# Delta rule: a 16-bit first correction of the triangular inverse, and decay columns as the bias of the exponential

## The chip, the cores and the metric

The kernel runs on one core of one Trainium2 chip. The metric is the device time of one execution in microseconds, as a median of several runs. Five engines work side by side: TensorE (PE in the profile, with its weight loads as PEld), VectorE (DVE), ScalarE (ACT), GpSimd (POOL), and SyncE (SP), which issues the DMA transfers.

## What is computed

One layer of an encoder trunk handles 2048 frames of a new stream ("prompt") and 64 frames of a running one ("sample"), 1024 channels wide. After a norm comes one input projection. One part of its columns feeds a gated delta rule with 4 heads of 128 channels, another a pooling group. Then come an output projection with a residual, a second norm, a SwiGLU feed-forward block and a last norm. The change is inside the delta rule, of which the reference says:

```
G = jnp.cumsum(g, axis=-1)
gamma = jnp.exp(jnp.where(lower_incl, G[..., :, None] - G[..., None, :], -jnp.inf))
kb = k * beta[..., None]
Lm = jnp.where(lower_strict, jnp.einsum('bhncd,bhnsd->bhncs', kb, k) * gamma, 0.0)
T = lax.linalg.triangular_solve(eye + Lm, eye, left_side=True, lower=True)
u = jnp.einsum('bhncs,bhnsv->bhncv', T, v * beta[..., None])
w = jnp.einsum('bhncs,bhnsk->bhnck', T, kb * jnp.exp(G)[..., None])
qk = jnp.einsum('bhncd,bhnsd->bhncs', q, k) * gamma
```

For each chunk of frames it needs the matrix gamma of decay factors, whose exponent is a difference of a row value and a column value of the running sum G, and the inverse T of a triangular matrix. The state is then carried from chunk to chunk.

## The kernel before, in words

**Two phases.** Phase 1 runs from the start to about 1000 us: input projection, delta rule, pooling and output projection, over four blocks of 512 prompt frames (block 0 also takes the 64 sample frames). Phase 2 is the feed-forward block, and nothing in it is touched.

**The large matrix products.** In phase 1, `project` (line 787) and `out_proj` (line 1289) multiply with three products for each pair of tiles, since weights and activations are split into a high and a low part (`wsplit`, line 529; type F32R). Their results lie in the PSUM tiles pp and pz, which rotate over PSM = 3 banks. VectorE (in block 0) or ScalarE (in the other blocks) brings the projection's results out of PSUM in `evict` (line 779).

**Fronts.** Each head of each block has two `Front` objects (line 868) of two 128-frame chunks each: 4 blocks x 4 heads x 2 = 32, and one more for the four sample heads together (`h is None`). A front prepares everything that doesn't depend on the running state, in `all` (line 921):

- keys are transposed and normed (tiles ptk, ktl, kn)
- `rowmm` (line 897) writes the row values of G into a PSUM bank, tile gb; ScalarE takes the exponential EG of it (line 948)
- onto the same bank go a mask by a bf16 matmul with idbf (line 955) and, by `negmm` (line 908), the negative column values: two F32R matmuls, for each chunk one, with seln as the moving operand. ScalarE's exponential of that, two chunks in one instruction, is Gam (line 961)
- GpSimd takes the identity off (Gst), and the products of keys and queries in bank gr are multiplied in (lines 965 to 972)
- the inverse is built up over seven levels in 16-bit arithmetic (tiles Um, py, Yt, pt, TV; lines 979 to 1001). Levels 0, 2 and 4 write a tile with the tag TV0, levels 1, 3 and 5 one with the tag TV1, and the last writes TV32 in 32 bits, with T and V as its halves
- two corrections follow. The residual F (tile pf and line 1008) is multiplied with V into bank px0, and T = V + that (lines 1010 to 1013); then F is multiplied with the new T into px1, and X = V + that (lines 1016 to 1020). These four matmul calls for each front have 32-bit operands. px0 and px1 are both shown as px_p (px_s for the sample front) in the profile.

**Heads.** `Head` (line 1032) then carries the state through the chunks (tiles pk, rhs, vn, po) and norms the result (osq, os). At most NLEV = 3 fronts have a set of level tiles and a bank at the same time.

**What sets the order.** Every instruction is first noted by `Machine` (line 59) with an estimated duration and then put in order by a greedy list scheduler, `issue` (line 183), for all engines at once. Fronts and heads are "hot" and go ahead of projection work. On TensorE, `pick` (line 281) takes 16-bit and plain 32-bit matmuls ahead of F32R ones, and holds them back for a moment while F32R work is at hand. Since it ranks by estimates, any change of the instructions can shift the order elsewhere too. All instructions of the program are issued from line 278, so the profile's groups are told apart by their tiles.

**Rows.** `rows` (line 1137) computes G and its exponentials for each block. A matmul with sel12 puts the running sums, frames on partitions, into the PSUM tile pc, and one exponential (line 1174) makes the tile EC from it.

The names with __ and a number in the profile are the same tiles, numbered.

## Time and profile before

| what | us |
|---|---|
| median of 3 runs | 2386.49 (2385.48 to 2387.06) |
| profiled execution | 2391.23 |
| its span, from first to last instruction | 2389.5 |
| TensorE busy | 2347.9 |
| VectorE busy | 1681.2 |
| ScalarE busy | 1217.8 |
| GpSimd busy | 971.1 |

The busy time of TensorE counts overlapped, modelled ends of matmuls, so it says where TensorE had something in hand, not that it ran at its peak. What one group of matmuls really takes is seen from the start of the group to the start of the next.

### The profile page before, as it was taken

The numbers are of one execution on the slowest core, as the hardware profiler recorded it, in microseconds if no ns is written. First come the engines' busy times: TensorE is split into PE (matmuls) and PEld (weight loads), VectorE is DVE, ScalarE is ACT, GpSimd is POOL, SyncE is SP. The second block draws the span as 40 slices with busy tenths as digits, with TensorE's granted clock in tenths as the row PEclk, the third lists the DMA queues.
The fourth block names the chain that finished last, engine by engine and source line by source line (L and its number), as shares of the span: only waits on it lengthen the run. The fifth ranks groups of instructions, "written<-read, shape, count | busy, mean of one in ns | idle before, by whom it ended". The sixth has DMA issues, their size and how long they took to land.

```text
span 2389.5 us, 41681 instructions
## 1 busy us (share of the span) xinstructions
PE 2347.9 (98%) x14803; PEld 2183.0 (91%) x14803; DVE 1681.2 (70%) x2963; ACT 1217.8 (51%) x2746; POOL 971.1 (41%) x1146
## 2 busy tenths in 40 slices
PE   9999999999999999999999999999999999999998
PEld 8999798778887878899999999999899999999998
DVE  7999875785577786787776763767566657666466
ACT  6666654564456464574454554553333554434334
POOL 1656442554356652264332226454233464222111
PEclk9999999999999999999999999999999999999999
DMA  7644566455555575999876778976755697566763
GB/s 267 224 166 137 184 224 220 143 168 189 177 184 177 165 192 171 320 370 338 294 284 225 280 264 260 309 260 238 278 192 178 199 350 247 174 211 210 260 207 115
DMA packets 228448, 540.57 MB, mean 226 GB/s; under 512 B 28304, under 2 KB 86672, under 8 KB 228240
## 3 DMA queue, kind: packets, MB, share of 16 engines
q1 hardware_dynamic: 228240, 537.92, 66.8%
q8 instruction: 116, 1.90, 0.3%
q14 instruction: 92, 0.75, 0.1%
HBM read 389.41 MB, written 148.41 MB: 225 GB/s over the span
## 4 chain that ended last, share of the span: by engine, by line
PE 83%; DVE 8%; ACT 3%; DMA 2%; issue 2%; POOL 1%; SPq 0%; DVEq 0%; POOLq 0%; ACTq 0%
PE px L278 19%; PE pp L278 14%; PE pz L278 12%; PE py L278 10%; PE d L278 8%; PE dx L278 6%; PE dy L278 3%; PE pk_p L278 2%; PE pt_p L278 1%; PE dz L278 1%; PE gr_p L278 1%; DVE y L278 1%; PE px_p L278 1%; DVE Yqk L278 1%; PE py_p L278 1%
## 5 line engine op out<-in xcount | busy, mean ns | idle before, releaser
L278 PE MATMUL pp<-h,wsp 128*128 128x512 f32 (+1 forms) x2480 | 562.1, 366 | 3.9 <-DVE h L278 2.8
L278 PEld LDWEIGHTS pp<-h,wsp 128*128 128x128 f32 x2480 | 402.6, 190 | 52.0 <-DVE h L278 3.9
L278 POOL TENSOR_TENSOR Um_p<-Gst_p,lmask 128x256 f16<-128x256 f32 x224 | 179.0, 813 | 108.1 <-PE py_p L278 79.3
L278 PE MATMUL pz<-op,wsp 128*128 128x512 f32 (+1 forms) x960 | 216.7, 366 | 2.5 <-ACT op L278 2.0
L278 PEld LDWEIGHTS pz<-op,wsp 128*128 128x128 f32 x960 | 155.8, 190 | 22.5 <-ACT op L278 2.5
L278 PE MATMUL d<-h,wsd 128*128 128x352 f32 x1056 | 169.6, 322 | 0.0
L278 PEld LDWEIGHTS d<-h,wsd 128*128 128x128 f32 x1056 | 168.3, 188 | 0.5 <-DVE h L278 0.5
L278 DVE TENSOR_TENSOR TV_p<-TV_p,pt_p 128x512 f16<-128x512 f16 (+1 forms) x192 | 128.5, 681 | 48.4 <-PE pt_p L278 43.1
L278 PE MATMUL px<-hA,ws 128*128 128x352 f32 x792 | 141.9, 324 | 0.3 <-DMA ws<-g 0.3
L278 PE MATMUL pz<-hB,ws 128*128 128x352 f32 x792 | 139.9, 322 | 0.3 <-DMA ws<-g 0.3
L278 PE MATMUL py<-hB,wsS 128*128 128x352 f32 x792 | 139.1, 322 | 0.3 <-ACT u L278 0.3
L278 PE MATMUL px<-hBT,wsS 128*128 128x352 f32 x792 | 137.6, 322 | 1.9 <-ACT g L278 1.9
L278 PE MATMUL px<-hBT,ws 128*128 128x352 f32 x792 | 137.9, 322 | 1.5 <-DVE u L278 1.5
L278 PE MATMUL px<-hA,wsS 128*128 128x352 f32 x792 | 137.4, 322 | 0.9 <-ACT g L278 0.9
L278 POOL TENSOR_TENSOR wrS<-wr,wrS 128x512 f32<-128x512 f32 x44 | 62.9, 1430 | 185.4 <-DMA wrS<-in_wu_dram 61.2
L278 PE MATMUL py<-hA,wsS 128*128 128x352 f32 x792 | 137.4, 322 | 0.0
L278 ACT ACTIVATE hr<-g 128x352 f32<-128x352 f32 x132 | 65.7, 498 | 132.3 <-DVE g L278 131.9
L278 PEld LDWEIGHTS px<-hBT,wsS 128*128 128x128 f32 x792 | 128.2, 188 | 2.5 <-ACT g L278 2.5
L278 PEld LDWEIGHTS px<-hA,ws 128*128 128x128 f32 x792 | 129.8, 189 | 0.7 <-DMA ws<-g 0.6
L278 PEld LDWEIGHTS px<-hBT,ws 128*128 128x128 f32 x792 | 128.0, 188 | 2.3 <-DVE u L278 2.1
L278 PEld LDWEIGHTS px<-hA,wsS 128*128 128x128 f32 x792 | 128.3, 188 | 1.2 <-ACT g L278 1.2
L278 PEld LDWEIGHTS pz<-hB,ws 128*128 128x128 f32 x792 | 128.7, 188 | 0.6 <-issue 0.6
(690 smaller groups left out, 5499.8 us busy)
## 6 DMA issues: line engine op xcount, KB each, us to landing
wsS<-gS SPq DMA_DIRECT2D x176, 512.0 KB, 4.7
ws<-g SPq DMA_DIRECT2D x132, 512.0 KB, 4.7
wsp<-wnd SPq DMA_DIRECT2D x126, 512.0 KB, 3.5
gS<-wsS SPq DMA_DIRECT2D x88, 512.0 KB, 5.3
g<-ws SPq DMA_DIRECT2D x66, 512.0 KB, 5.3
wnd<-wsp SPq DMA_DIRECT2D x42, 512.0 KB, 4.7
xd<-x2d SPq DMA_DIRECT2D x96, 176.0 KB, 4.0
wrd<-in_wd_dram SPq DMA_DIRECT2D x56, 256.0 KB, 4.3
```

The lines of the kernel that those rows point to most:

```text
L278: getattr(getattr(self.nc, op.eng), name)(*args, **kw)
```

## The change

Three things change.

1. In each prompt front the two `negmm` matmuls are dropped. The mask matmul closes the bank. The exponential that makes Gam becomes two ScalarE instructions of one chunk each, which take the negative column values as a bias of one value for each partition.
2. The bias comes from a new tile NG of each block: one more ScalarE instruction in `rows` copies the running sums out of pc with the factor -1. The sample front keeps its `negmm`.
3. In every front, the sample's too, ScalarE makes 16-bit copies of V and F in a tile VF, which has the tag TV0. The first correction (px0) multiplies these copies. The second (px1) still multiplies 32-bit operands.

```
-            else:
-                for c in range(2):
-                    at = self.off + c * C
-                    mm(ps[:, c * C : (c + 1) * C], G[:, at : at + C], seln[:, self.h, :].to_broadcast([P, C]),
-                       start=False, stop=c == 1, skip_group_check=True)
...
-            dd = gb if self.h is not None else self.ps(f"dd_{tag}")
-            mm(dd[:, : 2 * C], idbf, bc(negm2 if self.h is None else negm, 2, C), start=dd is not gb, stop=False,
-               skip_group_check=dd is gb)
-            self.negmm(dd)
-            if dd is not gb:
+            Gam = self.QKG = gt([P, 2, C], F32, "Gam", NOUT)
+            if self.h is None:
+                dd = self.ps(f"dd_{tag}")
+                mm(dd[:, : 2 * C], idbf, bc(negm2, 2, C), start=True, stop=False)
+                self.negmm(dd)
                 self.rowmm(dd, False)
-            Gam = self.QKG = gt([P, 2, C], F32, "Gam", NOUT)
-            act(Gam, two(dd), AF.Exp)
+                act(Gam, two(dd), AF.Exp)
+            else:
+                mm(gb[:, : 2 * C], idbf, bc(negm, 2, C), start=False, stop=True, skip_group_check=True)
+                for c in range(2):
+                    act(Gam[:, c], two(gb)[:, c], AF.Exp, bias=self.B.NG[:, self.c0 + c, self.h : self.h + 1])
...
             tt(F, F, two(pf), ALU.subtract)
+            VF = lev(F16, "TV0", "w", [P, 2, 2, C])
+            nc.scalar.copy(VF[:, 0], V)
+            nc.scalar.copy(VF[:, 1], F)
             yield LAT_F
             px = self.ps(f"px0_{tag}")
             for c in range(2):
-                mm(px[:, c * C : (c + 1) * C], F[:, c], V[:, c], start=True, stop=True)
+                mm(px[:, c * C : (c + 1) * C], VF[:, 1, c], VF[:, 0, c], start=True, stop=True)
...
-        act(EC[:, :nch, :], pc[:, : 12 * nch].rearrange("p (c t) -> p c t", t=12), AF.Exp)
+        pcs = pc[:, : 12 * nch].rearrange("p (c t) -> p c t", t=12)
+        act(EC[:, :nch, :], pcs, AF.Exp)
+        NG = B.NG = gp.tile([P, 4, NH], F32, tag="NG", name=f"NG{j}", bufs=2)
+        act(NG[:, :nch], pcs[:, :, :NH], AF.Copy, scale=-1.0)
```

More of the change, by code (lines that the diff above doesn't have):

```diff
@@ L910, in negmm @@
             G = self.B.Ghl
-            if self.h is None:
-                for h in range(NH):
-                    mm(ps[:, h * DEC : (h + 1) * DEC], G[:, SO : SO + P], seln[:, h, :].to_broadcast([P, DEC]),
-                       start=False, stop=False)
-            else:
-                for c in range(2):
-                    at = self.off + c * C
-                    mm(ps[:, c * C : (c + 1) * C], G[:, at : at + C], seln[:, self.h, :].to_broadcast([P, C]),
-                       start=False, stop=c == 1, skip_group_check=True)
+            for h in range(NH):
+                mm(ps[:, h * DEC : (h + 1) * DEC], G[:, SO : SO + P], seln[:, h, :].to_broadcast([P, DEC]),
+                   start=False, stop=False)
         def all(self):
```

## Prediction

> **What bounds the kernel now.** I read the page first: the share of each engine, the slices, the chain that ended last.

> ```profile
> span 2389.5 us, 41681 instructions
> ...
> PE 2347.9 (98%) x14803; PEld 2183.0 (91%) x14803; DVE 1681.2 (70%) x2963; ACT 1217.8 (51%) x2746; POOL 971.1 (41%) x1146
> ...
> PE 83%; DVE 8%; ACT 3%; DMA 2%; issue 2%; POOL 1%; SPq 0%; DVEq 0%; POOLq 0%; ACTq 0%
> ```

> TensorE has something in hand for 98% of the span and carries 83% of the last chain. An average can hide stages, so next come the stretches of phase 1, where all fronts lie (columns: stretch, its length, busy us of PE, PEld, DVE, ACT, POOL, clock, DMA share, GB/s).

> ```profile
> 50.00:250.00 200.00, 196.54 (x1579) 181.78 (x1578) 187.95 (x377) 128.02 (x335) 117.91 (x169) 1.00 0.55 182
> 250.00:480.00 230.00, 227.75 (x1492) 193.78 (x1491) 159.63 (x292) 127.22 (x312) 97.35 (x136) 1.00 0.59 190
> 480.00:710.00 230.00, 229.52 (x1366) 183.93 (x1365) 153.98 (x272) 117.75 (x297) 102.38 (x141) 1.00 0.54 176
> 710.00:876.00 166.00, 161.54 (x989) 130.26 (x987) 130.60 (x220) 102.74 (x258) 112.22 (x143) 1.00 0.57 179
> 876.00:970.00 94.00, 91.01 (x517) 73.17 (x517) 67.61 (x127) 45.91 (x113) 23.57 (x30) 0.98 0.64 184
> ```

> TensorE is without work for 3.5, 2.3, 0.5, 4.5 and 3.0 us of these, 13.6 us of 920. From 250 on, VectorE has a fifth to a third free, ScalarE 38% and more, and the DMA engines over a third. The first stretch, block 0, is different: VectorE is busy for 187.95 of 200 us there. A TensorE that gets faster soon meets VectorE in that stretch, and nowhere else. Who makes TensorE wait between 250 and 876 is in its waits (us in total, times, longest):

> ```profile
> PE pk_p L278 <- DVE Sp L278: 1.7, 1, 1.7
> PE pt_p L278 <- ACT Yt_p L278: 0.9, 2, 0.5
> PE gb_p L278 <- ACT ktl_p L278: 0.9, 2, 0.5
> ```

> These are the three longest, 3.5 us in 626. While a front waits for its next step, projection matmuls fill TensorE. So the fronts' own latency is covered, and time that is taken off TensorE should come off the span.

> **What the edits take off TensorE.** Durations of matmuls overlap, so I take start to start, from the order of time on TensorE (start, us, group, count):

> ```profile
> 668.41 0.28 PE L278 MATMUL py_p<-TV_p,Um_p 128*128 128x128 f16 x2
> 668.53 0.66 PE L278 MATMUL pf_p<-TV_p,Gst_p 128*128 128x128 f32 x4
> 669.03 0.27 PE L278 MATMUL gb_p<-negm,idbf 128*128 128x256 bf16 x1
> 669.06 0.41 PE L278 MATMUL gb_p<-seln,Ghl 128*128 128x128 f32 x2
> 669.31 1.16 PE L278 MATMUL pp<-h,wsp 128*128 128x512 f32 x4
> 670.30 1.03 PE L278 MATMUL gr_p<-Yqk 128*128 128x256 f32 x4
> 671.17 0.27 PE L278 MATMUL pt_p<-Yt_p,TV_p 128*128 128x128 f16 x2
> 671.28 0.28 PE L278 MATMUL pt_p<-TV_p,Yt_p 128*128 128x128 f16 x2
> 671.39 0.66 PE L278 MATMUL px_p<-TV_p,F_p 128*128 128x128 f32 x4
> 671.81 0.47 PE L278 MATMUL pp<-h,wsp 128*128 128x512 f32 x1
> ...
> 938.98 0.28 PE L278 MATMUL pt_p<-TV_p,Yt_p 128*128 128x128 f16 x2
> 939.07 1.18 PE L278 MATMUL pz<-op,wsp 128*128 128x512 f32 x4
> 940.09 0.38 PE L278 MATMUL pk_p<-Sp,Yqk 128*128 128x128 f32 x2
> ```

> *Column values.* A pair of seln matmuls takes 669.06 to 669.31, 0.25 us. Not all of it goes. Four projection matmuls that follow such a pair take 0.99 us (669.31 to 670.30), four that follow a 16-bit pair 1.02 (939.07 to 940.09): the seln pair already pays 0.03 us of the turn to F32R that the next matmul pays without it. That leaves 0.22 us for a pair; bounds 0.22 and 0.25.

> *First correction.* The pair of 32-bit products runs as four matmuls and takes 671.39 to 671.81, 0.42 us. Pairs of the same size in 16 bits take 0.12 (668.41), 0.11 (671.17) and 0.09 us (938.98). The difference is 0.30 to 0.33; I take 0.31.

> ```profile
> L278 PE MATMUL px_p<-TV_p,F_p 128*128 128x128 f32 x256 | 40.7, 279 | 1.8 <-DVE F_p L278 1.1 <-DVE TV_p L278 0.5
> L278 PE MATMUL gb_p<-seln,Ghl 128*128 128x128 f32 x64 | 14.2, 307 | 0.0
> ```

> 64 seln matmuls are 32 pairs: 32 x 0.22 = 7.0 us (to 8.0). The 256 of px_p are two corrections of 32 fronts at four each; one of the two becomes 16-bit, and the sample front's too: 33 x 0.31 = 10.2 us (9.9 to 10.9). Together 17.2 us (16.9 to 18.9).

> **What they add, and where it lies.** ScalarE gets a second exponential for each prompt front, two casts for each front, and one copy for each block. The nearest rows:

> ```profile
> L278 ACT ACTIVATE Gam_p<-gb_p 128x256 f32<-128x256 f32 x32 | 12.2, 385 | 1.6 <-PE gb_p L278 1.4
> L278 ACT ACTIVATE vn_p<-pk_p,kn_p 128x128 f32<-128x128 f32 x64 | 23.6, 369 | 45.2 <-PE pk_p L278 45.1
> L278 ACT CAST Yt_p<-py_p 128x256 f16<-128x256 f32 x192 | 68.5, 371 | 111.8 <-PE py_p L278 111.1
> L278 ACT CAST wsd<-wrdl 128x256 fp32r<-128x256 f32 x36 | 14.6, 406 | 33.0 <-PE dx L278 25.5 <-PE py L278 7.0
> L278 ACT ACTIVATE EC<-pc x4: 205/211/211, 42.9 to 724.5; 128x48 f32<-128x48 f32 x4
> ```

> Two instructions like vn_p (one value for each partition, 128 wide) less one like Gam: 2 x 369 - 385 = 353 ns, an upper end, since neighbours overlap. Casts are shown with a 16-bit output from PSUM (371) and with an SBUF source (406); the new ones have both traits, so 66 x 0.37 to 0.41. NG is as EC, 4 x 0.21. In all 11.3 + 24.4 to 27.1 + 0.8 = 37 to 39 us. In the five stretches ScalarE was busy for 521.6 of 920 us, 57%; that becomes 61%. I cost it at nothing on the way to the end: what hides it is the projection work that TensorE does meanwhile. VectorE, GpSimd, the DMAs and SP's queue get nothing and are passed by nothing.

> In a front, the cast of F (0.41) stands in the chain, and its product is 0.31 shorter. V's cast can run while pf is made. The second exponential adds at most 0.35 ahead of Gst on GpSimd, and the 0.25 of the seln pair is gone. So a front becomes 0.1 us longer by the first and up to 0.1 by the second. Behind a cast that waits for F on ScalarE's queue stand its other casts, the SiLU exponentials and the evictions that free the three pp banks. F is made by one VectorE instruction:

> ```profile
> L278 DVE TENSOR_TENSOR F_p<-F_p,pf_p 128x256 f32<-128x256 f32 x32 | 13.2, 414 | 3.4 <-PE py_p L278 1.6 <-PE pf_p L278 1.3 <-POOL F_p L278 0.4
> ```

> A wait of about that length, 0.4 us, is short beside a bank, which 24 projection matmuls fill in 24 x 0.25 = 6 us (1.02/4 for one). If the cover were gone, 32 x 0.2 = 6 us would be the price of the longer chain.

> [...]

> **The sum.** Block 0 holds nine fronts, eight and the sample's: 8 x 0.53 + 0.31 = 4.6 us come off TensorE where VectorE is 94% busy. TensorE would need 192 us for this stretch and VectorE 188, with waits for one another in between. I take half as lost, 2.3 us (bounds 0 and 4.6). The schedule is put in order anew, and fronts are a little longer; on 13.6 us of waits I add 1 (bounds -2 and 5). 17.2 - 2.3 - 1 = 13.9 us. The profiled execution took 2391.2 us, 1.7 of it outside the span, and would take 2377.3. It is 4.7 above the median of the three runs, and I take the same 13.9 off the median 2386.5: 2372.6 us. The bounds together give 18.9 + 2 = 20.9 and 16.9 - 4.6 - 5 = 7.3 us, so 2365.6 to 2379.2.

> **The rivals.**

> *Partly eaten.* The greedy order is drawn anew and waits grow by half of the 13.6 us: 17.2 - 4.6 - 6.8 = 5.8 us, 2380.7. For it: durations in the scheduler are estimates, and block 0 is tight. Against it: the waits are few and scattered, no single one recurs.

> *No change.* TensorE isn't really the bound, and the matmuls taken out were covered: 2386.5. [...] Doubled waits (17.2 - 4.6 - 13.6 = -1) would come to the same time.

> *Slower.* ScalarE sets the pace: its queue is in order, and each front's 1.15 us (37 to 39 over 33) delays Yt, the evictions or the silu behind it, so that TensorE runs dry. Wholly uncovered that is 38 - 17.2 = 21 us more, 2407; with three quarters uncovered 28 - 17 = 11, 2398. It turns slower once 17.2/38, 45%, is uncovered. For it: ScalarE is the engine that gets work, and seven levels of each front pass through it by Yt. Against it: ScalarE waited for TensorE and not the other way round (111 us before Yt against 0.9 us of TensorE for Yt between 250 and 876).

> **Chances.** A measurement of this kernel can tell about 0.2%, 4.8 us, from no change: faster is below 2381.7, slower above 2391.3. My forecast, in its bounds, has 0.68; partly eaten 0.15; still more gained than the bounds say 0.03; no change 0.09; slower 0.05. The first three make 0.86 for faster. The range is 2365 to 2382, the forecast's bounds and the partly eaten case.

> **What would show it.** Right: the group gb_p from seln is gone; px_p splits into 128 32-bit and 64 16-bit matmuls, TensorE has 64 + 66 fewer (14803 to 14673), and ScalarE 32 + 66 + 4 more (2746 to 2848); a 16-bit pair of px takes about 0.11 us from start to start; the stretch after block 0, with 24 fronts, shrinks by about 24 x 0.53 = 12.7 us, and block 0 by some 2; phase 2, from the first px<-hA on, is as long as before; TensorE's waits for px_p and Gst stay under a microsecond or two. Wrong: waits of TensorE for Yt, pp banks or px_p that recur front by front; a phase 2 of another length; block 0 as long as before with more waits for VectorE; or new 16-bit groups that take 0.2 us and more.

## The result and the profile after

| | before | after |
|---|---|---|
| median of 12 runs, us | 2387.86 (2385.48 to 2391.02) | 2384.09 (2381.23 to 2388.95) |
| profiled execution, its span, us | 2391.23, 2389.5 | 2387.10, 2385.3 |
| granted clock of the profiled execution | 0.996 | 0.993 |

The ratio is 0.9983, with a 95% interval of 0.9976 to 0.9991: 3.8 us or 0.17% faster, where 13.9 us were forecast. That is just inside what I had called no change, and 2 us above the range.

The page of after, its span and its engines:

```profile
span 2385.3 us, 41505 instructions
...
PE 2339.3 (98%) x14673; PEld 2168.3 (91%) x14673; DVE 1674.2 (70%) x2963; ACT 1246.9 (52%) x2848; POOL 968.7 (41%) x1146
```

The instructions are as forecast: 14673 on TensorE, 2848 on ScalarE, and ScalarE's busy time is up by 29 us, where 37 to 39 were reckoned. The groups (mean ns of one behind the busy us):

```profile
L278 ACT ACTIVATE Gam_p<-gb_p,NG 128x128 f32<-128x128 f32 x64 | 20.1, 374 | 1.8 <-PE gb_p L278 1.7
L278 PE MATMUL px_p<-TV_p,F_p 128*128 128x128 f32 x128 | 20.0, 279 | 0.2 <-DVE TV_p L278 0.2
L278 ACT CAST TV0w_p<-F_p 128x256 f16<-128x256 f32 x32 | 13.1, 410 | 13.9 <-DVE F_p L278 13.7
L278 ACT CAST TV0w_p<-TV_p 128x256 f16<-128x256 f32 x32 | 13.0, 406 | 11.4 <-DVE TV_p L278 11.3
L278 PE MATMUL px_p<-TV0w_p 128*128 128x128 f16 x64 | 9.0, 222 | 0.0
```

The seln group is gone and the first correction is 16-bit. TensorE never waited for it (0.0 us before px_p<-TV0w_p). So the work did leave TensorE. Where the time went is in the same stretches of phase 1 as before (length, busy us of PE, PEld, DVE, ACT, POOL, clock, DMA share, GB/s):

```profile
50.00:250.00 200.00, 193.41 (x1523) 177.22 (x1522) 185.65 (x374) 133.88 (x359) 118.33 (x172) 0.98 0.53 180
250.00:480.00 230.00, 229.60 (x1490) 194.40 (x1489) 160.50 (x302) 136.18 (x341) 94.88 (x136) 1.00 0.57 194
480.00:710.00 230.00, 229.36 (x1369) 183.62 (x1368) 154.91 (x278) 128.89 (x328) 106.89 (x147) 1.00 0.54 178
710.00:876.00 166.00, 161.53 (x940) 127.44 (x940) 130.24 (x215) 105.24 (x269) 106.07 (x138) 0.97 0.54 177
876.00:970.00 94.00, 90.31 (x514) 71.37 (x513) 70.50 (x132) 50.88 (x126) 24.88 (x31) 1.00 0.65 201
```

The column to look at is the clock: 0.98 and 0.97 where before had 1.00 and 1.00. I had read that column and not used it. In the waits of TensorE over the whole of after, the largest entry (us in total, times, longest) is

```profile
PE py_p L278 <- DVE TV_p L278: 5.1, 5, 2.6
```

where before had

```profile
PE py_p L278 <- DVE TV_p L278: 1.0, 3, 0.5
```

The longest of the five, 2.63 us, seen in the order of time on all engines:

```profile
714.54 1.06 POOL L278 TENSOR_TENSOR pw<-pw 128x524 f32<-128x524 f32 x1 [3.00 <-DMA od<-pd]
715.66 0.63 POOL L278 MEMSET Rt<- 64x643 f32 x1
716.33 2.78 DVE L278 TENSOR_SCALAR Rt<-Rt 4x128 f32<-4x128 f32 x4 [2.19 <-POOL Rt L278]
...
719.46 0.67 DVE L278 TENSOR_TENSOR TV_p<-TV_p,pt_p 128x512 f16<-128x512 f16 x1
720.16 0.68 DVE L278 TENSOR_TENSOR Ghl<-Rt,Ghl 32x512 fp32r<-32x512 f32 x1
720.18 0.37 PE L278 MATMUL py_p<-TV_p,Um_p 128*128 128x128 f16 x2 [2.63 <-DVE TV_p L278]
```

A pooling sum on GpSimd waits for a transfer. Behind it in GpSimd's queue stands the memset of Rt, behind that in VectorE's queue the row work on Rt, and behind that the TV of a front, for which TensorE stands ready. No instruction of the change takes part in these rows. That the scheduler's estimates put the queues in an order that the chip didn't keep up with is my reading of them.

What follows such a wait is in two short stretches around it (same columns):

```profile
715.00:720.00 5.00, 2.55 (x12) 1.83 (x11) 3.66 (x6) 1.31 (x2) 3.82 (x6) 0.98 0.71 249
720.00:725.00 5.00, 4.82 (x19) 3.91 (x19) 3.67 (x6) 1.74 (x6) 1.19 (x2) 0.50 0.14 56
```

For five microseconds TensorE runs at half clock, 0.50 (the whole stretch, from 719.85 us on, is 6.83 us long by the clock records of the trace). Another place, in the order of time on TensorE, shows the matmuls themselves:

```profile
86.68 0.27 PE L278 MATMUL py_p<-TV_p,Um_p 128*128 128x128 f16 x2 [1.28 <-DVE TV_p L278]
87.28 0.71 PE L278 MATMUL pf_p<-TV_p,Gst_p 128*128 128x128 f32 x4 [0.33 <-DVE TV_p L278]
...
89.23 2.51 PE L278 MATMUL pp<-h,wsp 128*128 128x288 f32 x9
91.54 0.51 PE L278 MATMUL ptk_p<-consts,Yqk 128*128 128x128 f32 x2
91.89 0.61 PE L278 MATMUL pf_p<-TV_p,Gst_p 128*128 128x128 f32 x4
92.25 1.18 PE L278 MATMUL pp<-h,wsp 128*128 128x288 f32 x7
93.27 0.28 PE L278 MATMUL px_p<-TV0w_p 128*128 128x128 f16 x2
```

After waits of 1.28 and 0.33 us, nine projection matmuls take 0.26 us each (89.23 to 91.54); a little later seven of the same take 0.15 (92.25 to 93.27). The clock records have half clock from 88.38 to 91.79. So these waits cost more than their length.

**The books of the two profiles.** The groups give 17.2 us less. Waits: the five stretches leave TensorE 15.8 us without work where it was 13.6; over the whole span, less the busy time on the pages, it is 46.0 us where it was 41.6, 4.4 more. Clock: 2389.5 x 0.004 = 9.6 us of full speed were withheld before, 2385.3 x 0.007 = 16.7 after, 7.1 more. Turns: counted in the order of time, TensorE leaves its F32R work (pp, pz, os, rpn and the products with selp and seln) for other matmuls 472 times up to the end of phase 1, before it was 449. A 16-bit pair alone between projection matmuls costs 0.19 us there and one in company about 0.10 (from the start of the group before to the start of the group behind, less the projection matmuls), so 23 turns are 2 us. -17.2 + 4.4 + 7.1 + 2 = -3.7; the spans differ by -4.2. The clocks are rounded to 0.001, which is 2.4 us, so the sum can't be closer than that.

### The profile page after: what moved, and what is told of

Same layout as the page of the kernel before. It is cut to its first block, busy times and chain, and to the rows that moved or that the text cites. A ratio compares the mean times of both kernels' runs of the same rounds, so it can differ in the third digit from the quotient of the medians.

```text
span 2385.3 us, 41505 instructions
## 1 busy us (share of the span) xinstructions
PE 2339.3 (98%) x14673; PEld 2168.3 (91%) x14673; DVE 1674.2 (70%) x2963; ACT 1246.9 (52%) x2848; POOL 968.7 (41%) x1146
## 4 chain that ended last, share of the span: by engine, by line
PE 82%; DVE 8%; DMA 3%; ACT 2%; issue 2%; POOL 1%; SPq 0%; DVEq 0%; POOLq 0%; ACTq 0%
PE px L278 19%; PE pp L278 14%; PE pz L278 12%; PE py L278 9%; PE d L278 8%; PE dx L278 6%; PE dy L278 3%; PE pk_p L278 2%; PE pt_p L278 1%; PE dz L278 1%; DVE y L278 1%; PE gr_p L278 1%; DVE TV_p L278 1%; PE py_p L278 1%; DVE Yqk L278 1%
## 5 line engine op out<-in xcount | busy, mean ns | idle before, releaser
L278 PE MATMUL pp<-h,wsp 128*128 128x512 f32 (+1 forms) x2480 | 573.3, 370 | 3.9 <-ACT h L278 1.2
L278 PEld LDWEIGHTS pp<-h,wsp 128*128 128x128 f32 x2480 | 406.3, 192 | 53.2 <-DVE h L278 3.0
L278 POOL TENSOR_TENSOR Um_p<-Gst_p,lmask 128x256 f16<-128x256 f32 x224 | 176.4, 801 | 120.5 <-PE py_p L278 91.4
L278 PE MATMUL pz<-op,wsp 128*128 128x512 f32 (+1 forms) x960 | 218.6, 367 | 4.4 <-ACT op L278 3.0
L278 PEld LDWEIGHTS pz<-op,wsp 128*128 128x128 f32 x960 | 155.6, 190 | 24.1 <-ACT op L278 3.6
L278 PE MATMUL d<-h,wsd 128*128 128x352 f32 x1056 | 169.7, 322 | 0.0
L278 PEld LDWEIGHTS d<-h,wsd 128*128 128x128 f32 x1056 | 168.4, 188 | 0.5 <-DVE h L278 0.5
L278 DVE TENSOR_TENSOR TV_p<-TV_p,pt_p 128x512 f16<-128x512 f16 (+1 forms) x192 | 128.9, 681 | 46.5 <-PE pt_p L278 45.6
L278 PE MATMUL px<-hA,ws 128*128 128x352 f32 x792 | 140.9, 322 | 1.8 <-DMA ws<-g 1.8
L278 POOL TENSOR_TENSOR wrS<-wr,wrS 128x512 f32<-128x512 f32 x44 | 63.0, 1432 | 194.7 <-DMA wrS<-in_wu_dram 96.6
L278 PE MATMUL px<-hBT,wsS 128*128 128x352 f32 x792 | 137.7, 322 | 4.0 <-ACT g L278 4.0
L278 PE MATMUL pz<-hB,ws 128*128 128x352 f32 x792 | 140.0, 322 | 0.9 <-DMA ws<-g 0.8
L278 PE MATMUL px<-hBT,ws 128*128 128x352 f32 x792 | 137.6, 323 | 2.0 <-DVE u L278 2.0
L278 PE MATMUL py<-hB,wsS 128*128 128x352 f32 x792 | 139.0, 322 | 0.0
L278 PE MATMUL px<-hA,wsS 128*128 128x352 f32 x792 | 137.5, 322 | 0.8 <-ACT g L278 0.8
L278 PE MATMUL py<-hA,wsS 128*128 128x352 f32 x792 | 137.6, 322 | 0.4 <-DMA wsS<-gS 0.4
L278 PEld LDWEIGHTS px<-hBT,wsS 128*128 128x128 f32 x792 | 128.3, 188 | 4.6 <-ACT g L278 4.6
L278 ACT ACTIVATE hr<-g 128x352 f32<-128x352 f32 x132 | 65.7, 498 | 126.4 <-DVE g L278 125.9
L278 PEld LDWEIGHTS px<-hA,ws 128*128 128x128 f32 x792 | 128.9, 188 | 2.2 <-DMA ws<-g 2.1
L278 PEld LDWEIGHTS px<-hBT,ws 128*128 128x128 f32 x792 | 127.9, 188 | 3.1 <-DVE u L278 2.9
L278 PEld LDWEIGHTS pz<-hB,ws 128*128 128x128 f32 x792 | 128.6, 188 | 1.5 <-ACT hB L278 1.1
L278 PEld LDWEIGHTS px<-hA,wsS 128*128 128x128 f32 x792 | 128.3, 188 | 1.4 <-ACT g L278 1.4
```

The lines of the kernel that those rows point to most:

```text
L278: getattr(getattr(self.nc, op.eng), name)(*args, **kw)
```

## The experiments

The theories: A, the saving is real, and the new order of the work, drawn by a greedy scheduler from estimates, takes most of it back in waits and clock; B, ScalarE's added work holds the fronts back; C, VectorE bounds block 0, or more generally time off TensorE is worth nothing. The 0.25 of `MARGIN` in the scheduler (line 1662) serves as a means to draw another order from the same instructions.

### One edit at a time, and the casts alone

The bias alone (the change without VF; px0 multiplies F and V):

> Only the decay columns as a bias; the first correction stays in 32 bits. By start-to-start times TensorE loses 32 x 0.22 = 7.0 us. Theory A (the matmuls' saving is real, and what the new order of the work adds in waits of TensorE and in stretches of half clock gives most of it back, whichever edit it comes from): the group from seln is gone, yet the time falls by less than 7 us or not at all, 2380 to 2390, and the rest is found in TensorE's waits and in its clock. Theory B (ScalarE's added work, above all the casts, holds the fronts back): there are no casts here, so the saving comes in full, about 2381. Theory C (block 0 is bound by VectorE): 24 of 32 fronts' saving, 5.3 us, all of it after block 0.

2380.35 us, ratio 0.9963 (0.9951 to 0.9976).

The 16-bit product alone (`negmm` and the one exponential as before):

> Only the first correction in 16 bits, with its casts; the column values stay matmuls. TensorE loses 33 x 0.26 to 0.31 = 8.6 to 10.2 us. Theory A: a fall of anything between 0 and 10 us, by how the new order falls out; the difference to 10 is found in waits and clock. Theory B: the casts cost about what the 16-bit products gain, 2384 to 2390. Theory C: 24 of 33 fronts' saving, 7 us, about 2381.

2389.92 us, ratio 0.9999 (0.9990 to 1.0008).

The kernel before with the casts and nothing else:

```
+            VF = lev(F16, "TV0", "w", [P, 2, 2, C])
+            nc.scalar.copy(VF[:, 0], V)
+            nc.scalar.copy(VF[:, 1], F)
```

> The kernel before with the two casts of each front added on ScalarE, 27 us of its time in all, and nothing reads them: the first correction still multiplies the 32-bit F and V, so no front's chain is longer. Theory B: slower by 5 to 15 us. Theory A: ScalarE has room; within 4 us of the kernel before, either way, by how the order falls out.

2388.74 us, ratio 1.0001 (0.9992 to 1.0010). 27 us more on ScalarE cost nothing that can be measured. That speaks against theory B as to load; the chain through the casts isn't in it.

The whole change with VectorE's casts:

```
-            nc.scalar.copy(VF[:, 0], V)
-            nc.scalar.copy(VF[:, 1], F)
+            nc.vector.tensor_copy(VF[:, 0], V)
+            nc.vector.tensor_copy(VF[:, 1], F)
```

> The whole change, but the casts are made by VectorE. Theory B: ScalarE is relieved of 27 us, and the time falls to 2375 or below. Theory C: block 0 gets longer by some 5 us, since VectorE has 14 us left there and gets 9 x 2 casts. Theory A: another draw of the order, between 2376 and 2388, with the difference in TensorE's waits and clock and none in the groups px_p and gb_p.

2379.24 us, ratio 0.9964 (0.9951 to 0.9976), 4.9 us below the whole change. By itself that speaks for B, or is another draw; the same casts in another order, further down, decide. Theory C's longer block 0 didn't come: between the row products of blocks 0 and 1 it took 213 us, where the change as made took 223. So far: the bias gives somewhat more than its 7 us, the 16-bit product nothing.

### Is TensorE's time the bound at all?

Both start from the bias alone. One leaves the product out, the other issues it twice:

```
-            px = self.ps(f"px0_{tag}")
-            for c in range(2):
-                mm(px[:, c * C : (c + 1) * C], F[:, c], V[:, c], start=True, stop=True)
-            tt(T, V, two(px), ALU.add)
+            tt(T, V, F, ALU.add)
```

> The kernel with the bias alone (2380.35 us) without the first correction's product at all: its 66 matmul calls are left out, T is V + F, and so the inverse is not corrected as in the reference; VectorE's sum stays, no casts. TensorE loses 33 x 0.44 = 14.5 us against the bias alone. If TensorE's matmul time sets the span one for one: about 2366. Theory A (the new order's waits and half-clock stretches take part of each saving): 2368 to 2378, with a lower granted clock than the 0.996 of the bias alone. If time off TensorE in the fronts is worth nothing below the bias alone's level (theory C, another engine or the fronts' latency is the bound from there on): within 4 us of 2380.

```
                 mm(px[:, c * C : (c + 1) * C], F[:, c], V[:, c], start=True, stop=True)
+            for c in range(2):
+                mm(px[:, (c + 2) * C : (c + 3) * C], F[:, c], V[:, c], start=True, stop=True)
```

> The kernel with the bias alone, the 32-bit product of the first correction issued twice: the second pair goes to the other half of its bank and is read by nobody. 33 x 0.44 = 14.5 us more on TensorE, nothing else. One for one: 2395. Theory A: 2388 to 2395, with a clock of 0.997 or more, since a busier TensorE has fewer waits. Theory C: within 4 us of 2380, since the fronts' products would lie beside other engines' work.

2369.22 us without it (ratio 0.9915, 0.9901 to 0.9928), 2390.16 with it twice (1.0003, 0.9994 to 1.0011). 14.5 us less on TensorE bring 11.1 us, 14.5 more cost 9.8. Theory C falls: TensorE's time in the fronts reaches the span. In these runs it is 0.7 to 0.8 of it, but each is also an order of its own, and the next section shows what that alone is worth. The clocks of the profiled executions are 0.996 without and 0.996 with it twice, the bias alone had 0.998; over all runs the medians are 0.996, 0.998 and 0.996. So the busier TensorE had the better clock, as theory A says, but the less busy one no worse than the bias alone.

### The same instructions in other orders

```
-MARGIN = {"tensor": 0.25,
+MARGIN = {"tensor": 0.30,
```

> The whole change with the same instructions in another order: the scheduler's margin behind TensorE results is 0.30 us and not 0.25. Theory A: the order is worth several us; a time between 2372 and 2390 that differs from 2384 by 3 us or more, with the difference in TensorE's waits, half-clock stretches and turns between kinds of matmul. Theory B (ScalarE's added work holds the fronts back): within 2 us of 2384, as ScalarE's work is the same.

> The kernel before with the same new margin, as the control of the run above: same instructions, another order. Theory A: also another time by some us, 2383 to 2395, in either direction. If the kernel before sat in an order that was chosen by trial, the time goes up, 2390 to 2398.

2373.97 us for the whole change (ratio 0.9933, 0.9919 to 0.9946) and 2383.24 for the kernel before (0.9969, 0.9957 to 0.9980). The ratios, here and below, are to the kernel before with its margin of 0.25. The same 14673 instructions on TensorE and 2848 on ScalarE took 10 us less in another order. Two more margins, 0.20 and 0.35:

> The whole change in a third order (margin 0.20). Theory A: what the change is worth on an average over orders is 14.5 us of TensorE's work or so (7.0 + 8.6 less the turns), passed on at 0.7 as with the product left out or issued twice, 10 us; in any one order it comes out some us above or below. So a time between 2368 and 2388, and 5 to 15 us below the kernel before in the same order. If the worth is really only the 4 us seen at first, this pair differs by 0 to 6.

> The kernel before in the third order (margin 0.20): its partner. 2380 to 2395, by theory A.

> The whole change in a fourth order (margin 0.35). As for the third: 2368 to 2388, 5 to 15 us below its partner by theory A, 0 to 6 if the change is worth only 4 us.

> The kernel before in the fourth order (margin 0.35): its partner. 2380 to 2395, by theory A.

With 0.20, 2375.77 (0.9946, 0.9933 to 0.9958) against 2384.64 (0.9983, 0.9974 to 0.9992); with 0.35, 2378.68 (0.9964, 0.9950 to 0.9978) against 2394.22 (1.0027, 1.0016 to 1.0037). And the bias alone in these three orders:

> The bias alone in the third order (margin 0.20), where the kernel before takes 2384.6 and the whole change 2375.8. Theory A (each edit is worth its TensorE time times 0.7 on an average over orders: 5 us for the bias, 6 for the 16-bit product): on an average over the orders the bias alone lies midway between the two, 2380 here, by some us either way. Theory D (the 16-bit product is worth nothing, whatever the order, since its turns and its lower clock eat it): equal to the whole change, 2376.

> The bias alone in the second order (margin 0.30), between 2383.2 and 2374.0. Theory A: about 2379. Theory D: about 2374.

> The bias alone in the fourth order (margin 0.35), between 2394.2 and 2378.7. Theory A: about 2386. Theory D: about 2379.

2378.72 (0.9958, 0.9946 to 0.9971), 2387.24 (0.9991, 0.9982 to 1.0000) and 2383.25 (0.9971, 0.9960 to 0.9981). All medians, us:

| margin | before | bias alone | whole change | whole less before |
|---|---|---|---|---|
| 0.25 (as made) | 2388.3 | 2380.35 | 2384.09 | -4.2 |
| 0.30 | 2383.24 | 2387.24 | 2373.97 | -9.3 |
| 0.20 | 2384.64 | 2378.72 | 2375.77 | -8.9 |
| 0.35 | 2394.22 | 2383.25 | 2378.68 | -15.5 |
| mean | 2387.6 | 2382.4 | 2378.1 | -9.5 |

(2388.3 is the median beside the runs of 0.30.) The order alone moves each kernel over some 9 to 11 us. On an average the bias gives 5.2 us and the 16-bit product 4.3 on top (5.7 and 3.4 by the ratios, since the kernels ran on several chips); by single orders the bias changed the time by between -11.0 and +4.0 us and the product by between -13.3 and +3.7. With four orders and this scatter the standard error of the product's 4.3 us (the spread of its four differences, 7.0 us, over the root of four) is 3.5, so the times alone don't exclude theory D of these runs, that it is worth nothing. The whole change's 9.5 us have a standard error of 2.3. As made, the whole change sat in the slowest of its four orders.

The traces tell more than the times. The span of a profiled execution can be divided in two: TensorE's work, as its busy time at full speed (busy time less half of what lies in stretches of half clock), and the rest, its waits and what half clock added. In us, for one execution each (that of the bias alone as made was its fastest):

| margin | work: before | bias alone | whole change | rest: before | bias alone | whole change |
|---|---|---|---|---|---|---|
| 0.25 (as made) | 2341.1 | 2334.0 | 2325.9 | 48.3 | 39.1 | 59.4 |
| 0.30 | 2337.2 | 2332.2 | 2325.0 | 44.7 | 53.2 | 46.5 |
| 0.20 | 2339.6 | 2334.4 | 2323.0 | 44.5 | 42.5 | 48.1 |
| 0.35 | 2340.0 | 2331.0 | 2324.0 | 56.2 | 45.9 | 51.9 |
| mean | 2339.5 | 2332.9 | 2324.5 | 48.4 | 45.2 | 51.5 |

The work falls in every order, by 5.0 to 9.0 us with the bias, by 7.0 to 11.4 with the product, by 15.0 with both on an average. That is the 17.2 of the forecast less 2 for the turns. Theory D's turns don't eat the product, then. Leaving it out or issuing it twice changed the work by -13.6 and +13.5 us against the bias alone, so nearly all of the 14.5 us reaches the work, one for one. If the work is the same in every execution, an estimate of the rest at the median times is 47 us without the product, 45 with it and 41 with it twice, and this rest made 0.7 to 0.8 of it. The rest moves over 12 to 14 us with the order, for each kernel; whether the change also adds to it (3 us on an average) isn't shown.

In order 0.30 the clock of after has no dent between 50 and 970 us; two of the lines:

```profile
50.00:250.00 200.00, 194.54 (x1540) 176.72 (x1539) 185.23 (x376) 135.39 (x360) 120.02 (x171) 1.00 0.55 183
...
710.00:876.00 166.00, 162.29 (x988) 128.76 (x987) 137.47 (x232) 108.17 (x277) 112.42 (x139) 1.00 0.61 181
```

Casts on VectorE in that order:

> The whole change with the casts on VectorE in the second order (margin 0.30), as a candidate for the best version. In the first order that was 5 us better than casts on ScalarE. Theory B (ScalarE's casts cost these 5 us): 2369. Theory A (that was another draw of the order): within 5 us of 2374 on either side, no better on an average of the two orders.

2385.29 us, ratio 0.9989 (0.9980 to 0.9998): 11.3 us worse than casts on ScalarE, where in the first order they were 4.9 better. Theory B falls with that: on an average of the two orders the casts on VectorE are 3.2 us slower, not faster.

### What a wait costs beyond its length

In 15 places of phase 2 of the kernel before, a small matmul waits for GpSimd sums whose time is hidden from the scheduler; two sums in one kernel, three in the other:

```
+        if f % 4 == 3:
+            s = tmp(f"slow{tag}")
+            machine.boost = BOOST
+            for i in range(2):
+                nc.gpsimd.tensor_tensor(out=s, in0=s if i else g1, in1=g1, op=ALU.add)
+                machine.ops[-1].lat = machine.ops[-1].occ = 0.05
+            mm(psg(f"slow{tag}")[:, :16], ones, s[:, :16], start=True, stop=True)
+            machine.boost = 0
```

> The kernel before with 15 waits of TensorE put into the second phase: at each a small matmul of 16 columns, read by nobody, has to wait for two GpSimd sums in a row, whose duration the scheduler doesn't know of. By the GpSimd rows of before (1.1 us for such a sum) TensorE should stand still for some 1.5 to 2 us at each, 22 to 30 us in all. If a wait costs only its own length: 22 to 30 us more and a clock as before, 0.997. If waits of this length bring a stretch of half clock (3.4 us long in the traces) most of the time: up to 15 x 1.7 = 26 us on top, and a clock down to 0.987.

> The same with three sums at each place: waits about 1.1 us longer, 17 us more in all than with two. If a wait costs only its own length: 17 us above that run and the same clock. If the half clock follows longer waits more surely: more than 17 us above it and a lower clock, down to 0.987.

The waits came out shorter than I had reckoned. TensorE's waits in phase 2, with two sums:

```profile
PE slow L278 <- POOL slow L278: 9.2, 14, 1.0
...
PE slow L278 <- DMA out_yT_dram<-y: 0.7, 1, 0.7
```

and with three:

```profile
PE slow L278 <- POOL slow L278: 23.9, 15, 1.9
```

With two: 2403.06 us (ratio 1.0064, 1.0049 to 1.0079), 15.9 more than before's 2387.2, of which the waits are 9.9 and the 15 small products, at 0.25 us from start to start, 3.8; 2.2 are left. The median clock of its runs is 0.997, that of before's runs beside it 0.998, and 0.001 x 2400 is 2.4 us. With three: 2421.97 (1.0145, 1.0128 to 1.0162), 18.9 more than with two, for 14.0 us more of waits, at a clock of 0.995: 0.002 x 2400 = 4.8 us, and 14.0 + 4.8 = 18.8. So, by medians of four runs, waits of 0.7 us cost their length and little more, and waits of 1.5 to 1.9 us up to a third more, in half clock that follows some of them. The waits are those of one execution each, and the two profiled executions bear out less: their spans differ by 11.9 us, of which TensorE's time without work is 10.8. With three sums, three of the 15 waits are followed by a stretch of half clock in the profile, 3 x 1.7 = 5.1 us for 23.9 us of waits; with two, none. One of the three, with the clock of the stretches before it, around it and after it:

```profile
1510.00:1515.00 5.00, 4.09 (x26) 3.80 (x24) 2.01 (x4) 3.42 (x9) 2.04 (x3) 1.00 1.03 399
1515.00:1520.00 5.00, 4.36 (x18) 4.36 (x19) 0.00 (x0) 1.58 (x4) 4.69 (x6) 0.66 0.53 199
1520.00:1525.00 5.00, 5.00 (x33) 5.00 (x32) 1.48 (x3) 1.70 (x4) 1.49 (x2) 1.00 0.73 213
```

The wait ends at 1515.64 in that run. A clock of 0.66 over 5 us is 3.4 us at half. The same kernel has a wait of 1.54 us that ends at 1600.57, and the clock of 1600 to 1605 is 1.00: not every such wait is followed by it. The last section says how far the traces settle which are.

In the trace of after, half clock came with waits that were shorter than its own stretches of 3.41 us. It began at 719.85 us within the wait of 2.63 us shown above, at 88.38 behind those of 1.28 and 0.33 us, and at 160.06 behind three of 0.40, 0.74 and 0.24 us. In the 3.41 us before these points TensorE was busy for 33, 53 and 59% of the time.

## Why the prediction was wrong, step by step

- **TensorE bounds phase 1, and what leaves it comes off the span.** Right. TensorE's work at full speed fell by 15.0 us on an average of four orders. Of 14.5 us, the runs without the product and with it twice passed on 0.7 to 0.8 to the time, and four orders passed on 9.5 of the 17.2; the difference lies in waits and half clock, which the forecast had at 1 us.
- **0.22 and 0.31 us for the pairs.** The groups did go. A 16-bit product in company takes what I said; alone among projection matmuls it pays for the turn, 0.19 us, where a 32-bit pair counted in the same way took 0.45 before, hardly more than in company. That is 0.26 and not 0.31, and part of the 2 us of turns.
- **ScalarE's added work is covered.** Right: casts at 406 and 410 ns, exponentials at 374, next to no waits of TensorE for them, and 27 us of casts alone cost nothing that could be measured.
- **Half of block 0's saving is lost on VectorE.** Wrong as a cause. As made, block 0 got longer, 40.2 to 263.2 us between the row products of blocks 0 and 1 where it was 41.6 to 260.6, but with more waits and half clock, not on a busier VectorE. The stretch of block 0 after,

```profile
40.00:263.00 223.00, 216.19 (x1634) 197.69 (x1635) 201.01 (x409) 148.50 (x389) 120.21 (x180) 0.96 0.53 179
```

and before:

```profile
41.00:260.00 219.00, 214.90 (x1674) 198.05 (x1674) 202.99 (x408) 143.35 (x365) 121.64 (x181) 0.99 0.55 182
```

TensorE is without work for 6.8 us there where it was 4.1, and half clock withheld 8.5 us where it was 1.7. VectorE is busy for 201.01 us where it was 202.99. So block 0 took 4 us more where 2 less were forecast, and the rest of phase 1 8.7 less where it was 12.7. Within another order of the same instructions (margin 0.35) it took 209 us and not 223:

```profile
42.00:251.00 209.00, 207.00 (x1614) 190.91 (x1615) 192.44 (x399) 144.45 (x379) 117.17 (x178) 0.99 0.57 190
```

VectorE was busy for 92% of it, so at 223 us it had been no wall.

- **"The schedule is put in order anew ... I add 1 (bounds -2 and 5)."** This is the step that failed. A new order is worth several us either way, with the same instructions: 2383 to 2394 for the kernel before, 2374 to 2384 for the whole change. As made it was 6 us worse than the mean of four. In the two profiles waits grew by 4.4 us and half clock by 7.1, 11.5 where I had added 1. The half clock is a term that I had put at nothing: I took the granted clock as given. Over its 12 runs the whole change had a median clock of 0.994; the runs of before beside most experiments have 0.997. The difference is 7 us of full speed. It belongs mostly to the order as made and not to the change as such: in the other three orders the medians are 0.994 to 0.996 for the whole change and 0.995 to 0.996 for before. Nor does the clock alone rank the orders, since before with the margin 0.30 runs at 0.995 and is 5 us faster than with 0.25. That the change came out at 3.8 us and not at 9 or 15 was the draw of its order.
- **The rivals.** The nearest was "partly eaten", 2380.7, with waits as its means; its chance was 0.15. Nothing bears out "slower" (ScalarE's pace) or "no change" for the reason that TensorE isn't the bound: leaving the product out and issuing it twice moved the time by -11.1 and +9.8 us. The casts took 520 and 422 ns on VectorE on an average, in the change with VectorE's casts, with 277 ns at the shortest and 1381 at the longest, and about 0.41 us on ScalarE. So some were faster on VectorE, but not the mean.
- **Phase 2 as long as before.** Nearly: 1393.5 us from the first px<-hA on, 1395.4 after.

What stays open: why a wait that leaves TensorE busy for about half of a window (last section) is or isn't followed by half clock (in after, 52% up to 248.81 us was, 50% up to 1040.70 us wasn't), and what the 16-bit product is worth in time to better than a few us. An order in which neither kernel has a long wait wasn't looked for beyond these four.

**The best version found** is the whole change with the margin of 0.30: 2373.97 us, 0.9933 of the kernel before. It is a draw among four, and another edit would draw again.

## What to carry to other kernels

Where a scheduler works from estimates, an edit changes the order everywhere: run the kernel before and the change in several orders, and compare means, before one believes or rejects an edit worth under 1%. Price matmuls from start to start and with their neighbours, and expect that sum less several us either way for the order: here four orders passed on 4 to 16 us of 17. Read TensorE's work at full speed apart from its waits and half clock; it told the edits' worth in one profile each, where the times needed many orders. Watch TensorE's waits of a microsecond and more and the granted clock beside them; what is lost there doesn't show in the busy share, which was 98% in both profiles.

## What the runs showed of the hardware

Such windows can be laid through the records of each trace, and TensorE's busy share in them counted. Between 36 us and the last 20 us of the 20 traces, each of the 49 windows in which TensorE was busy for less than 47.5% was followed by one at half clock; of 140 windows with 47.5 to 68.5%, 29 were; of 13336 with more, none (windows that were themselves at half clock are left out). In before and after alone it was 4 of 4, 5 of 17 and none of 1330. By these counts it matters how much of a wait falls into one window. In the run with three sums, a wait of 1.85 us that ended at 1128.40 lay across two windows and no half clock followed, while the one of 1.56 us that ended at 1515.64 lay within one. None of the 15 waits of 0.66 us on an average was followed by half clock in its profile.

Executions of the same program differ with the clock, though not by it alone: over the 12 runs of the whole change the spans go from 2379.5 us at a clock of 0.995 (and 2379.6 at 0.997) to 2387.2 at 0.992.
